# Moving the gate stage's stores from SyncE's queue to ScalarE's in a bidirectional GLA block

## The chip, the cores and the metric

The kernel runs on one core of a Trainium2 chip. The metric is the device time of one execution in microseconds (us). Each execution is timed from outside; the profile adds one execution that the hardware profiler recorded, with a span from its first to its last instruction.

The engines are named as in the profile: PE (TensorE, matmuls), PEld (its weight loads), DVE (VectorE), ACT (ScalarE), POOL (GpSimd) and SP (SyncE, which here does nothing but start transfers; its row is SPq). Every engine has its own instruction stream and works through it in order. An instruction that must wait for another engine or for a transfer holds up everything behind it on its own engine.

## What is computed

One layer of a hybrid encoder over 1024 tokens of width 1024, in float32:

```python
h = rmsnorm(x, norm_mix[l])
proj = h @ w_in[l]
q, k, v, r, lr_f, lr_b, u, g_a, g_b = jnp.split(proj, split_points, axis=-1)
...
o = o_fwd + o_bwd                      # bidirectional gated linear attention
...
y_a = o @ w_branch_gla[l]
pooled = multiscale_pool(u)
y_b = jnp.einsum('blgc,gcd->blgd', pooled, w_pool_group[l]).reshape(bsz, length, D_MODEL)
y_b = (y_b * pool_scale[l]).astype(x.dtype)
merged = jax.nn.sigmoid(g_a) * y_a + jax.nn.sigmoid(g_b) * y_b
x = x + merged @ w_out[l]
h2 = rmsnorm(x, norm_ffn[l])
gate, up = jnp.split(h2 @ w_ffn_in[l], 2, axis=-1)
x = x + (jax.nn.silu(gate) * up) @ w_ffn_out[l]
```

The stage that matters here computes three parts of `h @ w_in`: the pool input `u` (512 columns), the gate `g_a` and the gate `g_b` (1024 columns each). It also pools `u` (`multiscale_pool`), and applies the sigmoids.

## The kernel before

**Arithmetic.** A float32 operand is held as two fp32r tiles, hi and lo. ACT casts the hi part (`split_to`, L197), POOL or DVE subtracts to get the lo part (L198), and a matmul becomes three: hi·hi, hi·lo, lo·hi (`products`, L268 to L271). The large matrix products go by a Strassen–Winograd scheme: one unit has seven products, numbered p = 1 to 7, in place of eight. Each product is 12 matmuls of 128x128 by 128x512. The sums that the scheme needs are made by DVE (`combined`, L869, tiles `fs`) on the weights, and by DVE on the results (L1237, tiles `ga`).

**The gate stage** (390 to 602.6 us in the profile) runs ten units (`gate_units`): two for `u`, four for `g_a`, four for `g_b`. The loop is L1272 to L1310; its body goes over the seven products of a run. The runs overlap a little: product 4 of unit n−1 is done in run n, at position 2, and the last run has eight products. In each step:

- `gates_ahead.step()` prepares the weights of the product four ahead: ACT casts `wh`, POOL makes `wl`.
- `zs[of].run(p)` does the product. ACT copies three of the results from PSUM (L1232); the others are added by DVE (L1237) and then, for the gates, put through a sigmoid by ACT (L1240).
- At positions 1 and 2 the two raw weight blocks (`fraw`, 512 KB each, L861) of the next unit are loaded. They live in the same ring of buffers (`slot`) as the result rows `ga`, so such a load can wait for a row's store to land.
- `zs[of].store(...)` after products 7 and 4 only notes a store (`later`, L460): rows of `u` to `u_rows`, of gate A to `sa_out`, of gate B to `yb_out`. `flush()` (L463 to L465) issues the noted stores at position 4, and once more behind the loop.

Beside the products run two kinds of side work, which the function `pump` (L158) advances with every matmul group, one unit of its clock for three matmuls of 512 columns:

- **Pooling** (`pooling`, L1186 to L1202), begun in run 2 (`begin(pooling(), 4)`). For each of four channel groups: two loads of `u` (L1192, L1193), the windowed sums on DVE (`ws`, L1019 to L1033), a cast to `ph` by ACT (L1037), the lo part `pl` by DVE (L1039), and then two stores to `p_out` (L1200). The `u` buffers come from a ring of five (`t2`) that the `uph`/`upl` tiles share later. `load_pooled` reads the stored tokens back for the gate-B units.
- **Preparation for later stages** (`prepare_beside`, L608, and the generator `beside`, L572). In runs 0 to 6 it makes the sums of `w_out` (POOL, `wsum`, L600) and stores them as `t_wo`; from run 7 it prepares feed-forward units: sums on POOL (L600), a cast by ACT (L594, `uph`), the lo part by DVE (L585, `upl`), and two stores to `u_out` (L581). `finish_beside()` runs what is left at once; in the last run (the tenth) that is most of the units' work.

The last run also loads the blocks of the branch stage that follows (`load_block`, L1093, tiles `ob`; `line_load`, L1065, tiles `wraw`), which ACT casts to `dh` (L1080) and `wh`.

All transfers, loads and stores, are issued by SP, in the order in which the program writes them. A transfer whose data or buffer isn't ready holds up all transfers behind it. The compiled program also hands the transfers eight completion semaphores in turn, whichever engine issues them: one transfer is issued only when the eighth before it in the program has landed.

Of the kernel before, what the change touches and what calls it, by code (L numbers as in the profile page):

```python
# [43 lines left out]
PUT = 3  # L44
# [7 lines left out]
def kernel(  # L52
# [20 lines left out]
    nc = tc.nc  # L73
# [21 lines left out]
    def slot(dtype=F32, shape=(2, HALF), s="slot"):  # L95
        return slots.tile([P, *shape], dtype, tag="slot", name=name(s))

    def t2(width=HALF, dtype=F32, s="t"):
        return tmp.tile([P, width], dtype, tag="t2", name=name(s), padded_shape=[P, HALF + 2 * PAD])
# [10 lines left out]
    def as_f32(ap):  # L110
        return ap.bitcast(F32)
# [32 lines left out]
    side, aside = [], []  # L144
# [41 lines left out]
    def begin(gen, delay=0.0):  # L186
        side.append([gen, delay])

    def finish_side():
        while side:  # L190
            for _ in side[0][0]:
                pass
            side.pop(0)
# [269 lines left out]
    def flush(eng=nc.sync):  # L463
        while deferred:
            eng.dma_start(*deferred.pop(0))  # L465
# [21 lines left out]
    READY = 2  # L487
# [79 lines left out]
    def parts_for(src):  # L567
        if len(src.shape) == 2:
            return [t2(dtype=F32R, s=s)[:, :] for s in ("uph", "upl")]
        return [slot(F32R, s=s)[:, :, :] for s in ("trh", "trl")]  # L570

    def beside(jobs, every, put, lag):  # L572

        casts, differ = [None] * lag, None
        puts = [[] for _ in range(put)]
        while True:
            job = next(jobs, None)
            if not any((job, *casts, differ, *puts)):
                return
            for pair in puts.pop(0):  # L580
                nc.sync.dma_start(*pair)  # L581
            puts.append([])
            if differ:
                src, (hi, lo), dst = differ
                nc.vector.tensor_tensor(lo, src, as_f32(hi), op=ALU.subtract)  # L585
                if len(src.shape) == 2:
                    puts[-1] += [(dst[:, i, :], as_f32(t)) for i, t in enumerate((hi, lo))]
                else:
                    right.setdefault(dst, []).append((hi, lo))
            differ, cast = None, casts.pop(0)  # L590
            if cast:
                src, dst = cast
                parts = parts_for(src)
                nc.scalar.copy(parts[0], src)  # L594
                differ = src, parts, dst
            casts.append(None)
            if job:
                op, src, dst = job
                if op:
                    op()  # L600
                if src is not None:
                    casts[-1] = src, dst
                elif dst is not None:

                    puts[-1].append((dst, op.args[0]))
            yield every

    def prepare_beside(jobs, every, put=PUT, lag=1):  # L608
        aside.append([beside(chain(*jobs), every, put, lag), every])

    def finish_beside():
        while aside:
            for _ in aside[0][0]:
                pass
            aside.pop(0)
# [398 lines left out]
    def pooled(g, u, hi, lo):  # L1014
        width = WINDOWS[g]
        n = HALF + 2 * PAD
        for half in range(2):
            s = t2(n, s="ws")
            nc.vector.tensor_tensor(s[:, 1:n], u[half][:, : n - 1], u[half][:, 1:n], op=ALU.add)  # L1019
            yield 1  # L1020
            lo_p, hi_p, step = 1, n, 1
            while 2 * step < width:
                a = t2(n, s="ws")
                lo_p, hi_p = lo_p + step, hi_p - step
                nc.vector.tensor_tensor(
                    a[:, lo_p:hi_p], s[:, lo_p - step : hi_p - step], s[:, lo_p + step : hi_p + step], op=ALU.add
                )
                yield 1
                s, step = a, 2 * step
            e = slice(PAD, 2 * PAD) if half == 0 else slice(HALF, PAD + HALF)  # L1030
            nc.vector.tensor_tensor(s[:, e], s[:, e], edge[:, half, g, :], op=ALU.mult)
            body = slice(PAD, PAD + HALF)
            nc.vector.scalar_tensor_tensor(  # L1033
                s[:, body], s[:, body], 1.0 / width, u[half][:, body], op0=ALU.mult, op1=ALU.subtract
            )
            yield 1
            nc.scalar.copy(hi[:, half, :], s[:, body])  # L1037
            yield 1
            nc.vector.tensor_tensor(lo[:, half, :], s[:, body], as_f32(hi[:, half, :]), op=ALU.subtract)  # L1039
            yield 0.2  # L1040
# [5 lines left out]
    def line_load():  # L1046
        if len(loads) < len(line):
            loads.append(line[len(loads)][0]())
# [5 lines left out]
    def line_make():  # L1054
        n = len(made)
        if n < len(line):
            while len(loads) <= n:
                line_load()
            while len(begun_sums) <= n:
                line_sums()  # L1060
            made.append(line[n][2](loads[n]))
# [27 lines left out]
    def load_block(i, j):  # L1089

        ob[i, j] = [slot(s="ob") for _ in range(2)]
        for c in range(2):
            nc.sync.dma_start(ob[i, j][c][:, :, :], ob_out[i, 1 - j][:, 2 * c : 2 * c + 2, :])  # L1093
# [69 lines left out]
    p_out = dram.tile([GROUPS, 2, P, 2, HALF], F32, name="p_out")  # L1163
# [4 lines left out]
    def load_pooled(g):  # L1168

        while g not in stored:  # L1170
            next(side[0][0])
        pools[g] = [slot(F32R, s=s) for s in ("ph", "pl")]
        for n, t in enumerate(pools[g]):
            nc.sync.dma_start(as_f32(t[:, :, :]), p_out[g][n])

    def load_pool_weights(g):
        wpool["raw"] = s1((2 * P,), "wpr")
        nc.sync.dma_start(wpool["raw"][:, :], w_pool_group[0][g])

    def split_pool_weights(g):  # L1180
        wpool[g] = [small.tile([P, 2 * P], F32R, tag="s1", name=name(s)) for s in ("wph", "wpl")]
        split_to(*(t[:, :] for t in wpool[g]), wpool["raw"][:, :])
# [3 lines left out]
    def pooling():  # L1186

        for g in range(GROUPS):
            u = [t2(HALF + 2 * PAD, s="u") for _ in range(2)]
            nc.gpsimd.memset(u[0][:, :PAD], 0.0)  # L1190
            nc.gpsimd.memset(u[1][:, PAD + HALF :], 0.0)
            nc.sync.dma_start(u[0][:, PAD:], u_rows[g][:, : HALF + PAD])  # L1192
            nc.sync.dma_start(u[1][:, : PAD + HALF], u_rows[g][:, HALF - PAD :])  # L1193
            yield 4
            hi, lo = slot(F32R, s="ph"), slot(F32R, s="pl")
            for cost in pooled(g, u, hi, lo):
                yield POOLING * cost
            yield 4
            for n, t in enumerate((hi, lo)):
                nc.sync.dma_start(p_out[g][n], as_f32(t[:, :, :]))  # L1200
            stored.add(g)
            yield 1  # L1202

# [68 lines left out]
    for n, run in enumerate(gate_runs):  # L1272
        zs[n] = Gates(n)
        last = n == len(gate_units) - 1
        if n == 0:
            prepare_beside(map(output_jobs, range(4)), 2.8)
        if n == 7:
            finish_side()
            finish_beside()
            prepare_beside(map(unit_jobs, range(READY)), 3.1, 1, 2)  # L1280
        if last:
            finish_beside()
        for at, (of, p) in enumerate(run):
            if not gates_ahead.step() and at in (5, 7):
                line_make()
            zs[of].run(p)
            if at in (1, 2) and not last:
                gunits[n + 1].load()
            if p in (7, 4):
                zs[of].store(int(p == 4))  # L1290
            if at == 4:
                flush()
                if n == 2:
                    begin(pooling(), 4)
            if 5 <= n < 9 and at == 5:
                load_pool_weights(n - 5)
            elif n >= 6 and at == 2:
                split_pool_weights(n - 6)
            if n >= 6 and at == (0 if last else 3):
                load_pooled(n - 6)  # L1300
            if last and at == 1:
                load_block(0, 0)
                line_load()
                line_load()
                load_block(1, 0)
            elif last and at == 2:
                line_load()
                line_load()
                load_block(0, 1)
                load_block(1, 1)  # L1310
    finish_late()
    flush()

    U_BANKS = [ps_mm] * 3 + [ps_g]
    X_BANKS = [ps_g] * 4
# [472 lines left out]
    for at, p in enumerate(OUT_ORDER):  # L1788
# [4 lines left out]
        for i in range(CLOSE if closing else n_of):  # L1793
            n = at * n_of + i
# [50 lines left out]
```

## Time and profile before

| | us |
|---|---|
| runs of the kernel | 1408.82, 1405.72, 1407.31 (median 1407.31) |
| span of the profiled execution | 1405.0 |
| outside the span, at the median | 2.3 |
| gate stage in that execution | 390.0 to 602.6 |
| PE busy in the span | 1372.1 |

SP's stores of the gate stage are, by the answers of the trace on each tile: 16 `t_wo` (issue 323 ns at the median), 4 `u_rows` (424), 8 `p_out` (338), 8 `sa_out` (567), 8 `yb_out` (522) and 28 `u_out` (383 for `uph`, 320 for `upl`).

How to read the rows: a row of the timeline has start (us from the span's first instruction), duration, engine, line, operation, output<-input, shape, and in brackets the idle time before it with what ended it. A row of the waits has the waiting engine and line, what it waited for, total us, times, and the longest. A row of windows has start:end, length, then busy us and instructions of each engine shown, the granted PE clock, the DMA engines' busy share and GB/s.

### The profile page before, as it was taken

Reading aid. Unit: us, or ns where it says so; the run is one execution under the profiler, and the core shown is the slowest. Engines: PE = TensorE matmul, PEld = TensorE weight load, DVE = VectorE, ACT = ScalarE, POOL = GpSimd, SP = SyncE. Lnnn points to the kernel's source line nnn. Section 1 sums busy time; section 2 is a strip of 40 time slices with the busy share of each in tenths; the row PEclk is TensorE's granted clock in tenths of the full one; section 3 lists DMA queues with packets and bytes.
Section 4 is the critical chain, followed back from the end, with each engine's and each line's share of the span. In section 5 each row is a group of like instructions: output and inputs, shape, how many; then the busy total and the mean of one; then the engine's idle time right before and its main releaser. Section 6 shows DMA issues by size and latency. Waiting matters only on the chain.

```text
span 1405.0 us, 18577 instructions
## 1 busy us (share of the span) xinstructions
PE 1372.1 (98%) x6677; PEld 1155.0 (82%) x6677; DVE 842.7 (60%) x1073; ACT 623.5 (44%) x1119; POOL 751.0 (53%) x558
## 2 busy tenths in 40 slices
PE   7999999999999989999999999999999999999997
PEld 6889898988888768788887788888888888888876
DVE  6266757567745666677885865555655556343363
ACT  6364655554333444455356633333333334443253
POOL 3251616141288446567666076667666667464354
PEclk9999999999999999999999999999999999999999
DMA  6212413322377558998524555554444447976451
GB/s 192 76 46 61 135 52 114 98 69 75 121 214 250 195 173 273 334 406 291 185 75 151 186 188 173 173 167 148 140 146 148 140 155 255 387 259 222 165 227 72
DMA packets 167612, 243.62 MB, mean 173 GB/s; under 512 B 10936, under 2 KB 98016, under 8 KB 167520
## 3 DMA queue, kind: packets, MB, share of 16 engines
q1 hardware_dynamic: 167520, 242.45, 51.0%
q8 instruction: 52, 0.85, 0.2%
q14 instruction: 40, 0.33, 0.1%
HBM read 164.55 MB, written 77.86 MB: 173 GB/s over the span
## 4 chain that ended last, share of the span: by engine, by line
PE 67%; DVE 5%; issue 3%; DMA 2%; POOL 2%; ACT 2%; SPq 0%; POOLq 0%; ACTq 0%; DVEq 0%
PE ps L271 64%; DMA fraw<-in_w_in_dram 1%; POOL wl L198 1%; PE yb L271 1%; PE tp L959 0%; DMA gor<-g_out 0%; DMA wor<-t_out 0%; DVE fs L869 0%; PE op L800 0%; DVE ws L1033 0%; POOL fraw L600 0%; DVE x L1523 0%; POOL mg L1150 0%; DMA u_out<-uph 0%; ACT wh L197 0%
## 5 line engine op out<-in xcount | busy, mean ns | idle before, releaser
L198 POOL TENSOR_TENSOR wl<-fs,wh 128x512 fp32r<-128x512 f32 x120 | 166.1, 1388 | 172.1 <-ACT wh L197 138.6
L271 PE MATMUL ps<-gl,wh 128*128 128x512 f32 x616 | 239.8, 389 | 0.9 <-DVE gl L1439 0.9
L271 PE MATMUL ps<-gh,wh 128*128 128x512 f32 x616 | 240.3, 390 | 0.0
L271 PE MATMUL ps<-gh,wl 128*128 128x512 f32 x616 | 239.7, 389 | 0.0
L198 POOL TENSOR_TENSOR wl<-fraw,wh 128x512 fp32r<-128x512 f32 x90 | 128.9, 1432 | 60.1 <-ACT wh L197 57.3
L198 POOL TENSOR_TENSOR ol<-gor,oh 128x1024 fp32r<-128x1024 f32 (+1 forms) x42 | 100.1, 2389 | 93.2 <-ACT oh L197 87.5
L271 PE MATMUL ps<-hh,wh 128*128 128x512 f32 x376 | 149.6, 398 | 0.0
L271 PE MATMUL ps<-hh,wl 128*128 128x512 f32 x376 | 147.0, 391 | 0.0
L271 PE MATMUL ps<-hl,wh 128*128 128x512 f32 x376 | 146.7, 390 | 0.0
L198 POOL TENSOR_TENSOR wl<-raw,wh 128x512 fp32r<-128x512 f32 x47 | 64.5, 1389 | 146.6 <-ACT wh L197 135.7
L271 PEld LDWEIGHTS ps<-gl,wh 128*128 128x128 f32 x616 | 115.6, 188 | 25.0 <-DVE gl L1439 1.3
L271 PEld LDWEIGHTS ps<-gh,wl 128*128 128x128 f32 x616 | 115.6, 188 | 23.9
L271 PEld LDWEIGHTS ps<-gh,wh 128*128 128x128 f32 x616 | 115.6, 188 | 23.9
L271 PE MATMUL ps<-oh,oh 128*128 128x512 f32 x308 | 119.9, 389 | 1.1 <-DVE x L1767 1.1
L271 PE MATMUL ps<-ol,oh 128*128 128x512 f32 x308 | 119.9, 389 | 0.2 <-DVE ol L198 0.2
L271 PE MATMUL ps<-oh,ol 128*128 128x512 f32 x308 | 119.8, 389 | 0.0
L198 POOL TENSOR_TENSOR wl<-wraw,wh 128x512 fp32r<-128x512 f32 x56 | 89.8, 1631 | 45.1 <-ACT wh L197 45.0
L198 DVE TENSOR_TENSOR ol<-wor,oh 128x1024 fp32r<-128x1024 f32 (+1 forms) x42 | 62.0, 1496 | 54.0 <-ACT oh L197 46.7
L197 ACT CAST wh<-fs 128x512 fp32r<-128x512 f32 x120 | 73.7, 614 | 29.0 <-DVE fs L869 27.8
L271 PEld LDWEIGHTS ps<-hh,wl 128*128 128x128 f32 x376 | 70.7, 188 | 15.1
L271 PEld LDWEIGHTS ps<-hl,wh 128*128 128x128 f32 x376 | 70.9, 188 | 13.6
L271 PEld LDWEIGHTS ps<-hh,wh 128*128 128x128 f32 x376 | 70.8, 188 | 13.5
(251 smaller groups left out, 3183.0 us busy)
## 6 DMA issues: line engine op xcount, KB each, us to landing
fraw<-in_w_ffn_in_dram SPq DMA_DIRECT2D x44, 512.0 KB, 5.9
gor<-g_out SPq DMA_DIRECT2D x35, 512.0 KB, 6.1
raw<-in_w_in_dram SPq DMA_DIRECT2D x48, 256.0 KB, 3.2
g_out<-s SPq DMA_DIRECT2D x44, 256.0 KB, 2.3
fraw<-in_w_in_dram SPq DMA_DIRECT2D x20, 512.0 KB, 6.8
wor<-t_out SPq DMA_DIRECT2D x20, 512.0 KB
g_out<-g SPq DMA_DIRECT2D x33, 256.0 KB, 2.6
x<-in_x_dram SPq DMA_DIRECT2D x16, 512.0 KB, 5.7
```

Source lines behind the costliest of these rows:

```text
L197: nc.scalar.copy(hi, src)
L198: eng.tensor_tensor(lo, src, as_f32(hi), op=ALU.subtract)
L271: nc.tensor.matmul(ps, a[i], b[j], start=first and n == 0, stop=last and n == 2, skip_group_check=onto)
```

## The change

The stores of the gate stage are issued by ACT (`nc.scalar`) and no longer by SP (`nc.sync`): `t_wo` and `u_out` through the new argument `eng` of `beside`; `p_out` in `pooling()`; `u_rows`, `sa_out` and `yb_out` through the `flush` in the loop and the one behind it. The `p_out` store of the hi part also moves ahead of a `yield 4`, so that it comes 4 units of the side clock before that of the lo part. The loads stay on SP. The `flush()` ahead of the loop stays on SP too.

```diff
-    def beside(jobs, every, put, lag):
+    def beside(jobs, every, put, lag, eng):
...
             for pair in puts.pop(0):
-                nc.sync.dma_start(*pair)
+                eng.dma_start(*pair)
...
-    def prepare_beside(jobs, every, put=PUT, lag=1):
-        aside.append([beside(chain(*jobs), every, put, lag), every])
+    def prepare_beside(jobs, every, put=PUT, lag=1, eng=nc.sync):
+        aside.append([beside(chain(*jobs), every, put, lag, eng), every])
...
             for cost in pooled(g, u, hi, lo):
                 yield POOLING * cost
+            nc.scalar.dma_start(p_out[g][0], as_f32(hi[:, :, :]))
             yield 4
-            for n, t in enumerate((hi, lo)):
-                nc.sync.dma_start(p_out[g][n], as_f32(t[:, :, :]))
+            nc.scalar.dma_start(p_out[g][1], as_f32(lo[:, :, :]))
             stored.add(g)
             yield 1
...
         if n == 0:
-            prepare_beside(map(output_jobs, range(4)), 2.8)
+            prepare_beside(map(output_jobs, range(4)), 2.8, eng=nc.scalar)
         if n == 7:
             finish_side()
             finish_beside()
-            prepare_beside(map(unit_jobs, range(READY)), 3.1, 1, 2)
+            prepare_beside(map(unit_jobs, range(READY)), 3.1, 1, 2, nc.scalar)
...
             if at == 4:
-                flush()
+                flush(nc.scalar)
...
     finish_late()
-    flush()
+    flush(nc.scalar)
```

## The prediction

> **What bounds the kernel now.** I read the head of the page first, then the busy time of every engine by stretches of the gate stage.
>
> ```profile
> span 1405.0 us, 18577 instructions
> ...
> PE 1372.1 (98%) x6677; PEld 1155.0 (82%) x6677; DVE 842.7 (60%) x1073; ACT 623.5 (44%) x1119; POOL 751.0 (53%) x558
> ```
>
> ```profile
> 390.00:602.60 212.60, 206.31 (x895) 168.09 (x894) 126.41 (x148) 92.61 (x167) 135.29 (x103) 0.99 0.76 246
> ...
> 483.20:521.90 38.70, 33.00 (x133) 25.55 (x132) 28.10 (x37) 16.14 (x31) 16.51 (x14) 0.96 0.42 137
> ```
>
> The second fence holds windows: stretch, its length, then busy time and instructions of PE, PEld, DVE, ACT and POOL, the granted clock, the DMA share and GB/s. PE is the bound (98%), so a change in queues pays only where PE stands or runs slowly. The whole stage, 390.0 to 602.6 us, is changed. Nearly all that PE loses in it lies in one stretch, which the view of PE alone sets against a full one of the same length; under it are three rows of PE's timeline (start, duration, instruction, and in brackets the wait before it with what ended it).
>
> ```profile
> 400.00:438.70 38.70, 38.70 (x172) 1.00 0.86 256
> 483.20:521.90 38.70, 33.00 (x133) 0.96 0.42 137
> ```
>
> ```profile
> 512.06 0.39 PE L271 MATMUL ps<-trh,wl 128*128 128x512 f32 x1
> ...
> 514.72 0.50 PE L271 MATMUL ps<-trh,wh 128*128 128x512 f32 x1 [2.27 <-DVE ga L1237]
> ...
> 516.30 0.63 PE L271 MATMUL ps<-trh,wh 128*128 128x512 f32 x1
> ```
>
> Full, 172 matmuls go in 38.70 us, 0.225 each; here 133. The 39 that are missing are 39 × 0.225 = 8.8 us. The last rows show two ways of losing them: PE stands 2.27 us for VectorE, and restarts with a slower clock (a matmul of 0.63 us rather than 0.39). So the prize is about 8.8 us; there is little else to take, since the whole stage's 895 matmuls at 0.225 are 201.4 of its 212.6 us, which leaves 11.2 in all. Who makes VectorE late? Its own rows and ScalarE's:
>
> ```profile
> 479.12 0.71 DVE L1019 TENSOR_TENSOR ws<-u 128x527 f32<-128x527 f32 x1 [4.36 <-DMA u<-u_rows]
> ...
> 481.55 0.69 DVE L869 TENSOR_TENSOR fs<-fraw 128x512 f32<-128x512 f32 x1 [1.72 <-DMA fraw<-in_w_in_dram]
> ...
> 500.13 0.71 DVE L1019 TENSOR_TENSOR ws<-u 128x527 f32<-128x527 f32 x1 [4.46 <-DMA u<-u_rows]
> ...
> 504.65 0.69 DVE L869 TENSOR_TENSOR fs<-fraw 128x512 f32<-128x512 f32 x1 [3.81 <-DMA fraw<-in_w_in_dram]
> ```
>
> ```profile
> 484.23 0.63 ACT L1240 ACTIVATE ga<-ga 128x512 f32<-128x512 f32 x1 [7.76 <-DVE ga L1237]
> ...
> 507.33 0.63 ACT L1240 ACTIVATE ga<-ga 128x512 f32<-128x512 f32 x1 [9.94 <-DVE ga L1237]
> ```
>
> VectorE works in order. Four times it stands for a load (4.36 + 1.72 + 4.46 + 3.81 = 14.4 us); the additions behind it come late, so ScalarE's sigmoids do, and the weights and PSUM banks behind those. The loads are late because SP is:
>
> ```profile
> SPq L1200 <- ACT ph L1037: 46.1, 4, 15.2
> ...
> SPq L861 <- DMA sa_out<-ga: 8.7, 2, 5.3
> ```
>
> ```profile
> 474.60 0.41 SPq L1192 DMA_DIRECT2D u<-u_rows  x1
> ...
> 476.16 0.41 SPq L861 DMA_DIRECT2D fraw<-in_w_in_dram  x1
> 476.62 1.25 SPq L465 DMA_DIRECT2D sa_out<-ga  x2
> ...
> 494.04 0.34 SPq L1200 DMA_DIRECT2D p_out<-ph  x1
> ...
> 495.49 0.46 SPq L1192 DMA_DIRECT2D u<-u_rows  x1
> ...
> 497.08 0.43 SPq L861 DMA_DIRECT2D fraw<-in_w_in_dram  x1
> ```
>
> The first fence is the view of waits (total, times, longest): SP stood four times, 46.1 us together and 15.2 at worst, at a pooled-token store whose data ScalarE had not cast; at loads of fraw it stood twice, up to 5.3 us, for a buffer whose store had to land. The next u and fraw loads stand behind it in SP's program; nothing in their data needs that store.
>
> **The change part by part.** I sum against the profiled execution (1405.0 us of span), and add 1407.31 − 1405.0 = 2.3 us for what lies around it at the median of the runs.
>
> *Pooled stores and in-loop flush off SP: the gain.* SP no longer meets the wait of 15.2 us.
>
> ```profile
> 466.75 1.36 DVE L1039 TENSOR_TENSOR pl<-ws,ph 128x512 fp32r<-128x512 f32 x1 [1.73 <-ACT ph L1037]
> ...
> 486.29 1.02 DVE L1039 TENSOR_TENSOR pl<-ws,ph 128x512 fp32r<-128x512 f32 x1
> ...
> 487.95 1.68 DVE L1025 TENSOR_TENSOR ws<-ws 128x525 f32<-128x525 f32 x1
> ```
>
> The pooling of one group has last touched the buffers that the next group's u loads want at about 487.3 and 489.6 us (ends of the last two rows), against issues from 495.49: 6 to 8 us earlier is possible, more than VectorE's 4.46 us. The group before, by the same rule, could go from about 468.1 (the first row's end) rather than 474.60: 6 us against a wait of 4.36. The fraw of 497.08 needs the row buffer that the sa_out stores of 476.62 empty. That store moves behind ScalarE's sigmoid; were that still as late as 484.23 + 0.63, and the store as slow as before (SP stood up to 5.3 us for such a one just after issuing it, so I count 7), the buffer would be free near 492, 5 us ahead of 497.08 and more than the 3.81. Without the lateness it is freer still. So all four waits have cover, and I take the whole 8.8. Bounds: at most the 11.2 of the whole stage, at least about half, 4.4, if only the second pair of waits or only the first goes. VectorE itself has room: 28.10 us busy of 38.70.
>
> *What the stores cost ScalarE.* No store of before is issued by ScalarE, so their cost there is bounded by SP's rows (min/median/max in ns):
>
> ```profile
> L1200 SPq DMA_DIRECT2D p_out<-ph x4: 326/338/344, 456.3 to 520.2; - x4
> L581 SPq DMA_DIRECT2D u_out<-upl x14: 319/320/1283, 548.7 to 584.6; - x14
> L465 SPq DMA_DIRECT2D sa_out<-ga x8: 525/567/592, 459.2 to 523.8; - x8
> ```
>
> About 72 stores (16 t_wo, 4 u_rows, 8 p_out, 8 sa_out, 8 yb_out, 28 u_out) at 0.32 to 0.57 are some 28 us, on an engine that is busy 92.61 of 212.60: spread out, it hides in the 120 us of idle. Bounds: nothing, to 1.28 each where a queue is full. In order behind each store stand casts of weights (L197), copies (L1232) and sigmoids. Weights are prepared four products ahead, and a product is 12 matmuls × 0.225 = 2.7 us, so a delay under about 10 us is covered unless several fall together. The waits for data that move to ScalarE are short: it casts ph and uph itself, and the lo halves, POOL's sums and the rows are mostly done when their turn comes. Moving the hi store ahead of the `yield 4` costs nothing by the same cover.
>
> They do fall together in one place: the last run's `finish_beside()`.
>
> ```profile
> 573.00:586.00 13.00, 12.87 (x57) 10.25 (x56) 11.13 (x12) 6.88 (x12) 10.66 (x7) 1.00 0.94 357
> ```
>
> ```profile
> 573.14 0.33 SPq L581 DMA_DIRECT2D u_out<-upl  x1
> ...
> 584.60 0.39 SPq L581 DMA_DIRECT2D u_out<-upl  x1
> ```
>
> ```profile
> 578.18 0.62 ACT L594 CAST uph<-fraw 128x512 fp32r<-128x512 f32 x1 [0.77 <-DMA u_out<-upl]
> ...
> 583.17 0.62 ACT L594 CAST uph<-fraw 128x512 fp32r<-128x512 f32 x1 [1.07 <-POOL fraw L600]
> ```
>
> ```profile
> 591.30 0.50 PE L271 MATMUL ps<-trh,wh 128*128 128x512 f32 x1 [0.46 <-ACT ga L1232]
> ```
>
> From the first to the last of the quoted u_out rows are 13 stores at about 0.37, 4.8 us, and each cast of a unit waits for the store of five tiles before (the `<-DMA u_out` releaser) or for POOL. ScalarE falls 3 to 4 us behind, and here no slack is left: PE already waits 0.46 us for ScalarE's copy at 591.30. Of the delay I count 2.5 us as PE time, since the fraw load on SP at 565 to 567 gets out a microsecond or so sooner. Bounds 0 and 4.8.
>
> *The end of the stage.* The compiled program of before hands the DMAs of all queues eight completion semaphores in turn: each waits until the eighth before it has landed. Moved stores keep their places in that order, so ScalarE's now wait for SP's loads.
>
> ```profile
> 592.63 5.71 SPq L1093 DMA_DIRECT2D ob<-ob_out  x4
> 599.24 4.74 SPq L465 DMA_DIRECT2D yb_out<-ga  x4
> ```
>
> ```profile
> 592.40 0.63 ACT L1240 ACTIVATE ga<-ga 128x512 f32<-128x512 f32 x1 [1.16 <-DVE ga L1237]
> ```
>
> ```profile
> 602.60:676.00 73.40, 73.40 (x325) 1.00 0.88 333
> ```
>
> Four loads took SP 5.71 us and the yb_out stores went at 599.24. The first two of those now sit on ScalarE right behind the sigmoid that ends at 593.03, in front of the casts for the branch stage: up to 599.24 − 593.03 = 6.2 us of standing, with two issues about 7.2. The branch stage has no PE idle from 602.60 on (73.40 of 73.40), and the burst has by then put the stage 2.5 us back. I count 0.3; bounds 0 and 7.2.
>
> *The sum:* −8.8 + 2.5 + 0.3 = −6.0, so a span of 1399.0 and a time of **1401.3**.
>
> The Trainium skill, "DMA: Bandwidth & Descriptors", "Issuing engines are not separate DMA queues", speaks against the change: DMAs started by different engines run on the same 16 DMA engines, so spreading them saves only the issuer's time, usually little. By it alone the result would be the time of before. The row of 15.2 us is a wait in order, not issue, and the rule is not about that; I give it a small chance below.
>
> **The rivals.**
> - *The front gain without a bill* (the burst hides as the rest does): −8.8, 1398.5. For it: four products of cover. Against: the stall at 591.30 shows that this cover is used up there.
> - *A circle:* the fraw buffer waits for a store on ScalarE behind a sigmoid that waits for VectorE, which waits for fraw. Half of the gain (4.4) then stays, less 2.8 for the end: 1405.7. Against it is the estimate of 492 above.
> - *No gain at all:* transfers and not SP's place set when u and fraw land; 1407.3. Against it: the DMA share in the bad stretch is 0.42, where others run at 0.86. This is also what the rule cited above would give.
> - *Slower: ScalarE stands at the end.* The burst costs its full 4.8 and the standing at 593 its full 7.2: −8.8 + 12.0 = +3.2, so 1410.5. It decides once the burst and the wait together pass 8.8. For it: loads into a queue at 357 GB/s in the burst and ScalarE feeding both PSUM copies and weights. Against it: the two overlap.
>
> **How the numbers follow.** Forecast 0.42, no bill 0.22, circle 0.12, no gain 0.08, slower 0.16. A measurement of this kernel can tell about 0.2% from no change: 1404.5 to 1410.1. Faster is the first two, 0.64; same the next two, 0.20; slower 0.16. The likeliest alone spans 1398.9 to 1404 (burst 0 to 4.8 about its place). The range: the low end takes the bound of 11.2 with no bill, 1396.1; the top takes in circle and no gain with a bill of a microsecond, 1408.5, and leaves only the slower case out.
>
> **What would show it.** Right: u_rows loads issued from about 468 and 488; VectorE's waits of 4.36 and 4.46, 1.72 and 3.81 gone or under 1; PE in 483 to 522 at 38 or more; then a longer stall at about 582 to 585 (591.30 moved 8 us forward, plus the burst) released by ScalarE. The circle: `SPq L861 <- DMA sa_out<-ga` grows past its present share and PE keeps half of its stalls. Slower: ScalarE idle for 5 us or more at yb_out stores with PE standing at the start of the branch stage. It would be wrong if ScalarE's stores made the weight casts late anywhere before the burst, where I counted nothing.

## The result and the profile after

The changed kernel takes 1402.75 us (median of 11 runs, 1400.96 to 1404.74) against 1407.05 (median of 11, 1404.05 to 1408.82): a ratio of 0.9971, 95% interval 0.9962 to 0.998, some 2.8 to 5.3 us faster. The forecast was 1401.3, in a range of 1396.1 to 1408.5.

PE's windows of the changed kernel (stretch, length, busy us and matmuls, granted clock, DMA share, GB/s):

```profile
483.20:521.90 38.70, 38.70 (x172) 1.00 0.68 216
573.00:586.00 13.00, 9.64 (x35) 0.87 0.98 335
586.00:602.60 16.60, 16.60 (x74) 1.00 0.94 352
602.60:676.00 73.40, 73.40 (x326) 1.00 0.85 319
```

and two of the same windows of the kernel before:

```profile
573.00:586.00 13.00, 12.87 (x57) 1.00 0.94 357
586.00:602.60 16.60, 16.14 (x71) 1.00 1.02 370
```

The bad stretch is full: 172 matmuls where there were 133. All 8.8 us are back. A new hole stands in 573 to 586: 35 matmuls where 13.00 / 0.225 = 58 would fit, 23 × 0.225 = 5.2 us. The kernel before lost (58 − 57) + (74 − 71) = 4 matmuls, 0.9 us, in these two stretches. So −8.8 + 5.2 − 0.9 = −4.5 us, which agrees with the medians (−4.3). The two spans differ by 5.5 (1405.0 to 1399.5); 0.8 of that is there already when the gate stage begins, ahead of anything the change touches, and says nothing about it.

How the gain came, in SP's, VectorE's and ScalarE's timeline of the changed kernel:

```profile
463.75 0.32 SPq L1192 DMA_DIRECT2D u<-u_rows  x1
467.41 0.32 SPq L1193 DMA_DIRECT2D u<-u_rows  x1
467.78 9.08 SPq L861 DMA_DIRECT2D fraw<-in_w_in_dram  x2
484.72 0.34 SPq L1192 DMA_DIRECT2D u<-u_rows  x1
487.17 0.34 SPq L1193 DMA_DIRECT2D u<-u_rows  x1
487.60 0.39 SPq L861 DMA_DIRECT2D fraw<-in_w_in_dram  x1
```

```profile
475.39 1.81 DVE L1019 TENSOR_TENSOR ws<-u 128x527 f32<-128x527 f32 x1 [1.36 <-POOL u L1191]
...
494.47 1.81 DVE L1019 TENSOR_TENSOR ws<-u 128x527 f32<-128x527 f32 x1 [1.29 <-POOL u L1191]
```

```profile
471.76 0.62 ACT L1037 CAST ph<-ws 128x512 fp32r<-128x512 f32 x1 [0.98 <-DVE ws L1033]
472.41 0.33 ACTq L1198 DMA_DIRECT2D p_out<-ph  x1
```

The u loads that went at 474.60 and 495.49 go at 463.75 and 484.72. VectorE's waits of 4.36 and 4.46 us for them are gone; waits of 1.36 and 1.29 are left in their place, and those are for GpSimd, which clears the margin of the `u` buffer, and no longer for a DMA. On ScalarE the store stands right behind the cast of its own data (it is listed as ACTq) and waits for nothing.

And the new hole, in the timelines of the changed kernel. The first fence is PE's, the second ScalarE's, the third VectorE's; the fourth is a row of ScalarE in the kernel before.

```profile
578.83 0.50 PE L271 MATMUL ps<-trh,wh 128*128 128x512 f32 x1 [3.36 <-ACT ga L1232]
...
580.77 0.63 PE L271 MATMUL ps<-trh,wh 128*128 128x512 f32 x1
```

```profile
574.89 0.62 ACT L594 CAST uph<-fraw 128x512 fp32r<-128x512 f32 x1 [0.45 <-DMA u_out<-upl]
574.92 0.34 ACTq L581 DMA_DIRECT2D u_out<-uph  x1
575.30 0.54 ACTq L581 DMA_DIRECT2D u_out<-upl  x1
575.93 0.68 ACTq L581 DMA_DIRECT2D u_out<-uph  x1
577.30 0.33 ACTq L581 DMA_DIRECT2D u_out<-upl  x1
577.67 0.62 ACT L197 CAST wh<-fraw 128x512 fp32r<-128x512 f32 x1 [2.16 <-DVE upl L585]
578.20 0.58 ACT L1232 COPY ga<-ps 128x512 f32<-128x512 f32 x1
```

```profile
576.58 0.69 DVE L585 TENSOR_TENSOR upl<-fraw,uph 128x512 fp32r<-128x512 f32 x1 [1.41 <-DMA u_out<-uph]
```

```profile
584.22 0.58 ACT L1232 COPY ga<-ps 128x512 f32<-128x512 f32 x1
```

PE needs the copy at 578.20, which frees its bank. In ScalarE's order that copy stands behind the burst's casts and stores. Just ahead of it ScalarE waits 2.16 us, because the store at 577.30 needs a lo part; VectorE makes that part late, at 576.58, because it has waited 1.41 us for an earlier `u_out` store to land. By its place in ScalarE's order the copy is the one that the kernel before makes at 584.22, where PE didn't stand at all. The two parts of the hole are the stall (3.36) and the slow clock after it (0.63 us a matmul).

### The profile page after: what moved, and what is told of

Read it like the earlier page. It is cut to its first block, busy times and chain, and to the rows that moved or that the text cites. A ratio compares the mean times of both kernels' runs of the same rounds, so it can differ in the third digit from the quotient of the medians.

```text
span 1399.5 us, 18553 instructions
## 1 busy us (share of the span) xinstructions
PE 1369.9 (98%) x6677; PEld 1155.1 (83%) x6677; DVE 843.4 (60%) x1073; ACT 624.1 (45%) x1119; POOL 749.3 (54%) x558
## 4 chain that ended last, share of the span: by engine, by line
PE 69%; DVE 4%; DMA 2%; issue 2%; POOL 2%; ACT 1%; ACTq 0%; SPq 0%; POOLq 0%; DVEq 0%
PE ps L271 67%; DMA u_out<-uph 1%; POOL wl L198 1%; PE tp L959 0%; DMA gor<-g_out 0%; DMA wor<-t_out 0%; DVE upl L585 0%; PE op L800 0%; DMA ph<-p_out 0%; DVE x L1523 0%; PE yb L271 0%; POOL n3rs L1506 0%; POOL mg L1150 0%; POOL gl L1439 0%; ACT wh L197 0%
## 5 line engine op out<-in xcount | busy, mean ns | idle before, releaser
L271 PEld LDWEIGHTS ps<-hh,wl 128*128 128x128 f32 x376 | 70.6, 188 | 15.2
```

The source lines that it names most:

```text
L271: nc.tensor.matmul(ps, a[i], b[j], start=first and n == 0, stop=last and n == 2, skip_group_check=onto)
```

## The experiments

All ratios are to the kernel before, with their 95% intervals. The first four runs take the change apart by its groups of stores.

**units_on_sp**: the changed kernel, with the u_out stores back on SP.

```diff
-prepare_beside(map(unit_jobs, range(READY)), 3.1, 1, 2, nc.scalar)
+prepare_beside(map(unit_jobs, range(READY)), 3.1, 1, 2)
```

> The changed kernel, with the u_out stores alone put back on SP. Theory (the pooled stores on ScalarE bring 8.7 us, the u_out stores on ScalarE in the burst cost about 4.4): PE busy 38.7 of 38.7 in 483.2 to 521.9, no PE stall of 3.4 us for the copy L1232 near 578, ratio to before 0.994 (about 1398.5 us). Rival (ScalarE is held at the end by the yb_out stores, not by the u_out stores): the stall of 3 us or more stays, ratio 0.997. Second rival (SP with the u_out stores delays its fraw loads again, so that nothing is won): ratio 0.997 with a stall released by VectorE.

Measured: 0.9945 (0.9931 to 0.9959), 1399.96 us. The bad stretch stays full, and the hole is gone: the only stall of PE for a copy is 0.73 us at 584.49, at the place where the kernel before stood 0.46.

**pooled_alone**: the kernel before, with nothing but the `pooling()` part of the change.

```diff
+            nc.scalar.dma_start(p_out[g][0], as_f32(hi[:, :, :]))
             yield 4
-            for n, t in enumerate((hi, lo)):
-                nc.sync.dma_start(p_out[g][n], as_f32(t[:, :, :]))
+            nc.scalar.dma_start(p_out[g][1], as_f32(lo[:, :, :]))
```

> The kernel before, with only the pooled-token stores on ScalarE (the hi store ahead of the yield). Theory (SP's wait at these stores is the whole of the front loss): PE busy 38.7 of 38.7 in 483.2 to 521.9, the end of the stage as in the kernel before, ratio 0.994. Rival (the sa_out rows of the deferred stores hold SP next, since they wait for sigmoids): half of the gain, PE about 36 in that stretch, ratio 0.997.

Measured: 0.9949 (0.9936 to 0.9961), 1400.13 us. Its windows:

```profile
483.20:521.90 38.70, 38.70 (x172) 1.00 0.58 190
521.90:560.00 38.10, 38.10 (x168) 1.00 0.80 248
560.00:573.00 13.00, 11.27 (x49) 1.00 1.01 353
```

Eight stores moved do the whole of the front. The last row shows what becomes late next: 49 matmuls for 58, in waits for the pooled tokens read back (`[1.07 <-DMA ph<-p_out]` and 0.65 for `pl` in PE's rows). The t_wo, u_rows, sa_out and yb_out stores on ScalarE (units_on_sp has them, pooled_alone doesn't) make no difference that these intervals could show.

**pooled_on_sp**: the changed kernel, without the `pooling()` part (the same diff the other way).

> The changed kernel, with only the pooled-token stores back on SP. Theory: SP stands some 15 us at p_out again, PE about 33 of 38.7 in 483.2 to 521.9, and the burst at the end still costs about 4: ratio 1.003. Rival (any of the stores that leave SP gives the loads their way): PE 36 or more in that stretch, ratio 0.999 or less.

Measured: 1.0027 (1.0018 to 1.0037). SP stands up to 16.7 us at these stores again (42.9 us in four times), PE is busy 34.30 us with 146 matmuls in the bad stretch, and later it stalls 3.82 us for ScalarE's copy, until 588.93.

**units_alone**: the kernel before, with only the u_out stores on ScalarE (and the argument `eng` that this takes).

```diff
-prepare_beside(map(unit_jobs, range(READY)), 3.1, 1, 2)
+prepare_beside(map(unit_jobs, range(READY)), 3.1, 1, 2, nc.scalar)
```

> The kernel before, with only the u_out stores on ScalarE. Theory (costs add): the front stretch as before at 33 of 38.7, and a stall of PE of about 3 us with a slow clock behind it in the burst: ratio 1.003. Rival (the burst's stall comes from the earlier loads of the changed kernel, not from these stores): no such stall, ratio 1.000.

Measured: 1.0016 (1.0007 to 1.0025), less than the 1.003 that was expected. The stall is there, 2.62 us until 586.65, but no slow clock behind it. So the two parts nearly multiply: 0.9949 × 1.0016 = 0.9965, against 0.9971 for the whole change. The gain is the pooled stores', the cost the u_out stores', and each holds with and without the other.

The next three ask why the u_out stores on ScalarE cost time. My first theory was the wait for VectorE's lo part that is seen above at 577.67, taken by itself.

**units_lo_on_sp** and **units_hi_on_sp**: the changed kernel with one of each pair of u_out stores on SP.

```diff
-            for pair in puts.pop(0):
-                eng.dma_start(*pair)
+            for n, pair in enumerate(puts.pop(0)):
+                (nc.sync if put == 1 and n % 2 else eng).dma_start(*pair)
```

(`n % 2 == 0` in the second.)

> The changed kernel, with the u_out stores split: hi parts (cast by ScalarE itself) from ScalarE, lo parts (made by VectorE) from SP. Theory (in the burst ScalarE stands for VectorE's lo part in front of the weight cast and the copy L1232): the stall of PE near 578 falls under 1.2 us, ratio 0.995. Rival (the work of issuing 28 stores, 0.3 to 1.2 us each, is what delays ScalarE): half of the stores leave, the stall falls to about 1.8, ratio 0.996.

> The other half: the changed kernel with hi parts of the u_out stores from SP and lo parts from ScalarE. Theory (the wait for the lo part): the stall near 578 stays at about 3 us, ratio 0.997. Rival (issue work): as with the lo parts on SP, about 1.8, ratio 0.996.

Measured: 0.9958 (0.9945 to 0.997) with the lo parts on SP, 0.9947 (0.9935 to 0.996) with the hi parts on SP. With lo on SP, PE stands 0.35 and then 1.31 us for ScalarE, together near the rival's 1.8. With hi on SP, where ScalarE still meets every lo part, it stands 0.90 us, and ScalarE's wait for a lo part is down to 1.1. The theory had asked for a stall of 3 there, so it falls as it stood. The rival, issue work, asked for 1.8 in both, and in this one it isn't met either.

**units_put2**: every u_out store one step of its generator later, all on ScalarE.

```diff
-prepare_beside(map(unit_jobs, range(READY)), 3.1, 1, 2, nc.scalar)
+prepare_beside(map(unit_jobs, range(READY)), 3.1, 2, 2, nc.scalar)
```

> The changed kernel with every u_out store one step of its generator later (put 2 in place of 1), all still on ScalarE, as many instructions as before. Theory (ScalarE meets the store before VectorE has made the lo part): the part is ready by then, the stall near 578 falls under 1.5 us, ratio 0.995. Rival (issue work, or the stores' landing, which frees the five buffers, is what counts): the stall stays or grows, ratio 0.997 or more.

Measured: 1.0089 (1.0075 to 1.0103), 1420.72 us. Giving the lo part more time made it some 17 us worse (1.0089 against 0.9971), with as many instructions. The waits between 560 and 600 us (total, times, longest) and ScalarE's timeline of this kernel say why:

```profile
DVE upl L585 <- DMA u_out<-uph: 23.0, 7, 6.8
...
PE ps L271 <- ACT ga L1232: 16.4, 3, 13.8
ACT uph L594 <- DMA u_out<-upl: 15.3, 5, 6.2
```

```profile
582.91 0.62 ACT L594 CAST uph<-fraw 128x512 fp32r<-128x512 f32 x1 [2.17 <-DMA u_out<-upl]
582.94 0.33 ACTq L581 DMA_DIRECT2D u_out<-uph  x1
583.30 0.45 ACTq L581 DMA_DIRECT2D u_out<-upl  x1
585.69 0.62 ACT L594 CAST uph<-fraw 128x512 fp32r<-128x512 f32 x1 [2.15 <-DMA u_out<-upl]
585.77 0.33 ACTq L581 DMA_DIRECT2D u_out<-uph  x1
586.19 0.39 ACTq L581 DMA_DIRECT2D u_out<-upl  x1
588.83 0.62 ACT L594 CAST uph<-fraw 128x512 fp32r<-128x512 f32 x1 [2.53 <-DMA u_out<-upl]
```

This is a loop: cast, issue the stores, wait 2.2 to 2.5 us until one lands, cast again, 2.8 to 3.1 us a pair. The hi and lo parts live in a ring of five buffers, so a new part waits until the store of five tiles before has landed; and that store now can't leave before ScalarE has come to it in order, behind its own casts. On SP a store stood behind no cast. The new theory is the ring, and the next three runs are for it.

**ring6**: the changed kernel with a sixth buffer.

```diff
-    tmp = ctx.enter_context(tc.tile_pool(name="tmp", bufs=5))
-    small = ctx.enter_context(tc.tile_pool(name="small", bufs=5))
+    tmp = ctx.enter_context(tc.tile_pool(name="tmp", bufs=6))
+    small = ctx.enter_context(tc.tile_pool(name="small", bufs=4))
```

> The changed kernel with six t2 buffers in place of five (and, to make room, four s1 buffers in place of five, which may cost a little anywhere). New theory (a loop through the ring: a cast or a lo part waits until the store of five tiles before has landed, and that store now stands in ScalarE's order behind the casts): VectorE's waits for u_out<-uph in 560 to 600 us fall from 5.5 us to under 2, the stall of PE near 578 from 3.4 to about 1, ratio 0.995. Rival (the issue work of the stores, or the wait for the lo part alone): the stall stays at about 3, ratio 0.997.

Measured: 0.9939 (0.9926 to 0.9951), 1400.33 us. The waits in 560 to 600 us, of the changed kernel:

```profile
DVE upl L585 <- DMA u_out<-uph: 5.5, 3, 2.9
...
PE ps L271 <- ACT ga L1232: 3.4, 1, 3.4
...
ACT uph L594 <- DMA u_out<-upl: 1.3, 2, 0.9
```

and with the sixth buffer:

```profile
ACT uph L594 <- POOL fraw L600: 2.0, 2, 1.0
...
PE ps L271 <- ACT ga L1232: 1.0, 1, 1.0
...
ACT uph L594 <- DMA u_out<-uph: 0.4, 2, 0.3
```

VectorE's wait for a landing is gone (0.4 us on ScalarE is left), the casts wait for POOL's sums as in the kernel before, and PE's stall is 1.0, with all 28 stores still on ScalarE. ScalarE's waits for a lo part (2.2 and 1.6 us in the changed kernel) are gone with it, so they were a link of the loop and not a cost of their own. Slower landing by itself isn't it either: at the median the hi stores take 2.8 us from issue to landing in the kernel before, 3.8 in the changed one and 4.5 with the sixth buffer, where the stall is the smaller. So the loop through the ring made some 2.4 of the 3.4 us. The 1.0 that is left was not taken apart; four stores still stand between the last cast and the copy. Other tiles use the six buffers too, and the s1 buffers were not changed by themselves, so the ratio 0.9939 is not shown to be the loop's alone.

**put2_ring6**: units_put2 with the same edit of the two pools.

> The run with every u_out store one step later, with six t2 buffers (and four s1 buffers). Theory (ring): one more buffer is worth about half a step, and the stall of 13.8 us near 590 falls to 6 or less, ratio 1.002 or less. Rival (the late stores cost this by themselves): stall about 14, ratio 1.009.

Measured: 0.9997 (0.9987 to 1.0007). The stall of 13.8 falls to 6.4 us, a little over the 6 that was expected. The sixth buffer is worth 1.0089 − 0.9997, about 13 us, here.

**units_on_pool**: the changed kernel with the u_out stores on GpSimd.

```diff
-prepare_beside(map(unit_jobs, range(READY)), 3.1, 1, 2, nc.scalar)
+prepare_beside(map(unit_jobs, range(READY)), 3.1, 1, 2, nc.gpsimd)
```

> The changed kernel with the u_out stores on GpSimd, a third queue that holds neither loads nor casts. Theory (ring): GpSimd makes the sums that the casts wait for, so its stores stand in order behind the lo parts and the loop closes through GpSimd in ScalarE's place: a stall of 2 us or more in 570 to 590, ratio 0.997. Rival (any queue off ScalarE that has no loads is free): stalls under 1, ratio 0.994.

Measured: 1.0073 (1.0059 to 1.0086). The direction is the ring's, the size isn't: a stall of 9.39 us where I had said 2 or more, and 1.0073 for 0.997. The answer on the tile u_out of this kernel:

```profile
L581 POOL DMA_DIRECT2D u_out<-uph x14: 539/559/753, 542.9 to 590.9; - x14
...
  ACT uph L594: 28.9, 10
  DVE upl L585: 23.1, 7
```

and of the changed kernel, with the stores on ScalarE:

```profile
L581 ACTq DMA_DIRECT2D u_out<-uph x14: 321/332/1117, 539.3 to 575.9; - x14
...
  DVE upl L585: 9.0, 5
  ACT uph L594: 4.5, 4
```

(After each issue row: who waited for u_out, in us and times.) The hi stores issued by POOL cost it 559 ns each at the median, not 332, and hi and lo stores took 6.1 us to land, where those from ScalarE took 3.8 (hi) and 2.7 (lo). POOL itself stood 7.6 us for lo parts and 2.9 for casts ahead of these stores, and it makes the weights' lo parts as well: PE also stood 2.78 us for one of those, until 565.20. All of this can lengthen the loop or the time; how much each adds was not told apart.

**no_hoist**: units_on_sp, with the hi store of the pooled tokens behind the `yield 4` again.

```diff
-            nc.scalar.dma_start(p_out[g][0], as_f32(hi[:, :, :]))
             yield 4
+            nc.scalar.dma_start(p_out[g][0], as_f32(hi[:, :, :]))
```

> The changed kernel with the u_out stores on SP, and the hi pooled store behind the yield again, next to the lo store. Theory (the place of the store within ScalarE's order is without effect, only the queue counts): PE 38.7 of 38.7 in 483.2 to 521.9, ratio 0.9945 as with the hi store ahead. Rival (moving the hi store ahead is part of the gain): PE under 38, ratio 0.996 or more.

Measured: 0.9942 (0.993 to 0.9955), the same as units_on_sp. Moving the hi store ahead is no part of the gain.

**next_u_first** asks whether the gain needs a second queue at all: the kernel before, all stores on SP, with the next group's u loads written ahead of this group's stores.

```diff
...
+        u = load_u(0)
+        yield 4
         for g in range(GROUPS):
...
+            if g + 1 < GROUPS:
+                u = load_u(g + 1)
             yield 4
             for n, t in enumerate((hi, lo)):
                 nc.sync.dma_start(p_out[g][n], as_f32(t[:, :, :]))
```

(`load_u` holds the clearing and the two loads of one group, that stood at the head of the loop. The `yield 4` behind them there is left for the first group alone.)

> The kernel before, all stores on SP, with the u loads of the next group written ahead of the pooled-token stores of this group. Theory (order in SP's queue is the cause, the engine is not): VectorE's waits of 4.36 and 4.46 for u go, those for fraw, which stays behind the stores, do not; PE about 36 of 38.7 in 483.2 to 521.9, ratio 0.997 to 0.998. Rival (it takes a second queue): PE 33 to 34 there, ratio 1.000.

Measured: 0.9976 (0.9965 to 0.9987), 1403.28 us, PE 36.44 of 38.70 in the bad stretch. Order in SP's queue alone brings about half of what pooled_alone brings. I had expected the fraw waits to stay; they fell from 5.5 us to 1.0 between 460 and 525 us. What is left is one stall of 2.26 us and the slow clock after it. No load stands behind that stall: VectorE had waited 1.73 us for ScalarE's cast `ph`. Why it costs PE here and not in pooled_alone was not looked into.

## Why the prediction was right, and where it was off

- **The front gain, 8.8 us: right in mechanism; the size holds for the executions that were profiled.** The stretch is full, VectorE's four waits for loads are gone (two waits of 1.3 us for GpSimd are in their place, a little over the 1 that I had allowed), and pooled_alone and pooled_on_sp put it on the pooled stores. The u loads went at 463.75 and 484.72, each ahead of the 468 and 488 that I had named: only the second of the two buffers comes free as late as that. The size is partly luck: units_alone runs the same program up to there and misses 29 matmuls in the stretch (143 for 172), 6.5 us, where the profiled execution of the kernel before misses 39; most of the difference is the slow clock after the stall at 514.72, which units_alone doesn't have at the same stall.
- **The circle through sa_out** did not cost anything, but one of the two signs that I had named for it came. The sa_out stores waited behind the sigmoid as I had feared (it came at 480.89 rather than 484.23), and SP's wait for their landing at the fraw loads grew from 8.7 us (5.3 at the longest) to 14.9 (7.8). The other sign, PE keeping half of its stalls, did not come. The fraw loads now start early enough that VectorE waits for none of them between 460 and 525 us.
- **The stores' cost when spread out, nothing: right.** units_on_sp keeps 44 of the 72 stores on ScalarE and is as fast as pooled_alone.
- **The burst, 2.5 us: a stall for one of ScalarE's copies behind the burst was right; which copy, and the size, were not.** I expected the stall at 582 to 585, at the copy of 590.66 that releases PE at 591.30. It ended at 578.83, two copies earlier. The new hole is 5.2 us; less the 0.9 that the kernel before lost here, 4.3, near the upper bound of 4.8. Three things were missing. I had the ring of five in the text as a wait beside POOL's pace, but did not close it: with the stores on the casting engine, store and cast pace each other, and ring6 takes 2.4 of the 3.4 us of stall away. I had also taken the lo parts to be mostly done when ScalarE comes to their stores; the one at 577.30 cost it 2.16 us. And I priced a stall only by its length; after 3.36 us the clock was slow for some nine matmuls, each about 0.2 us longer, 1.6 to 1.8 us more.
- **The end of the stage, 0.3: nothing.** ScalarE did stand for loads (4.85 us ahead of a cast `dh` at 601.79), but PE is full from 586 to 676. The rival that ends slower needed the full burst and this wait as PE time; the burst came near its bound, the wait cost PE nothing.
- **The page's rule.** The Trainium skill, "DMA: Bandwidth & Descriptors", "Issuing engines are not separate DMA queues", says that spreading issuers saves only issue time. The runs differ: 0.9949, some 7 us, from eight stores whose issue costs 0.33 us each, 2.6 in all. What was saved is an in-order wait of 15.2 us, which the rule doesn't weigh; next_u_first, which saves no issue time and uses one queue, got 0.9976.

The sum of my terms was −6.0; with the measured ones it is −8.8 + 4.3 + 0 = −4.5. Both measured terms hold some 1.6 us of slow clock that another execution need not have, so that they meet the medians (−4.3) this closely is partly luck. The versions in which the loop is open or wider (units_on_sp, units_hi_on_sp, ring6, no_hoist; 0.9939 to 0.9947) are faster than both kernels; among the four the intervals overlap.

## What to carry to other kernels

A store in an in-order queue ahead of loads costs what its data is late, not what its issue takes; look for the longest wait on the queue's row, and move that store alone, or write the loads ahead of it. Before a store goes to the engine that makes its data, ask what its landing frees: where it frees a buffer that the same engine needs for its next piece, cast, store and landing become one loop, and the ring must hold a landing more. A burst is where that shows, and one buffer there can be worth more than the choice of queue.

## What the runs showed of the hardware that I had not expected

The slow clock doesn't follow from a stall's length alone. The kernel before and units_alone run the same program up to 515 us and stall at the same place for VectorE, 2.27 and 2.28 us. In the kernel before, the matmul at 516.30 takes 0.63 us, as the prediction shows; in units_alone none does:

```profile
515.04 0.50 PE L271 MATMUL ps<-trh,wh 128*128 128x512 f32 x1 [2.28 <-DVE ga L1237]
...
516.54 0.39 PE L271 MATMUL ps<-trh,wh 128*128 128x512 f32 x1
```

Elsewhere it is the same. In next_u_first the slow clock came after a stall of 2.26 us (0.68 of full clock in a window of 5 us around its end); in units_alone a later stall of 2.62 us had none (first matmul 0.50, the next ones 0.40, granted clock 1.00). PE's windows of these two kernels, next_u_first first:

```profile
490.00:495.00 5.00, 4.29 (x12) 0.68 1.02 309
```

```profile
586.00:595.00 9.00, 8.35 (x37) 1.00 1.00 376
```

The Trainium skill, "TensorE: Matmul & The Clock Gate", "What's actually happening", tells of an activity window of about 3.4 us that runs freely. If the place of a stall in that window counts, the same stall can have either outcome, as these rows show; no run here was made to test it. Its section "HAM oscillation — how this bites in real kernels" warns of gaps of PE over about 3.4 us; here 2.26 and 2.27 us were enough.
